# A hybrid-attention transformer block: where a gated product, four convolutions and nine operand splits stand

## The chip, the cores and the metric

The kernel runs on one core of a Trainium2 chip. The metric is the device time of one execution in microseconds; the median of several executions is given. TensorE is called PE here, with PEld for its weight loads; VectorE is DVE, ScalarE is ACT, GpSimd is POOL, and SP issues nearly all DMAs.

## What is computed

One transformer block over 512 tokens of 1024 features in float32: a modulation from a conditioning vector, a norm, a wide projection, a mixer of three kinds of heads, an output projection, a second norm and a gated feed-forward layer. Cut to what matters here:

```python
hn = (_rms(x, norm1_g[l]) * (1 + sc1) + sh1).astype(x.dtype)
proj = (hn @ w_in).astype(jnp.float32)
fq, fk, fv, ff, mq, mk, mv, mi, mf, mo, bq, bk, bv = jnp.split(proj, idx, axis=-1)
qk = jax.nn.silu(_causal_conv(jnp.concatenate([mq, mk], axis=-1), ml_conv_w, ml_conv_b))
mq, mk = jnp.split(qk, 2, axis=-1)
h_ml = _mlstm(_to_heads(mq, ML_HEADS), _to_heads(mk, ML_HEADS), ...)
...
gate, up = jnp.split(hn @ w_gate_up[l], 2, axis=-1)
x = x + g2 * ((jax.nn.silu(gate) * up) @ w_down[l])
```

The convolution has four taps along time, one weight per channel. There are four mLSTM heads, handled as two pairs, and 2816 feed-forward columns.

## The kernel before

Every float32 product is made of three products of split operands: a high part h (rounded, written by ACT) and a low part l = x - h (a subtraction), as `mm3` (hh, hl, lh) on PE. A weight tile therefore costs one ACT copy and one subtraction before PE can use it.

**Order of issue.** The tile framework places each engine's instructions itself while the program is built, by priority in the order of the text and by an estimate of when their inputs are ready; an instruction that stands late in the text may be placed early, where its engine would otherwise stand idle. What it has placed, an engine works off strictly in that order. A wrapper, `_InOrder`, can chain the instructions of an engine in the order of the text: while `in_order["V"][0]` and `in_order["S"][0]` are 1, those of DVE (`V`) and ACT (`S`) keep that order among themselves. What is issued after the switch is 0 again may still be placed between members of the chain. `SY` (the DMA issues) is chained from the feed-forward part on.

**First part.** After the norm, four 512-column products for the convolution (`gT` to `qkz[0..3]`; tiles 0 and 2 are the first pair of heads, 1 and 3 the second). Then come the projection groups of `add_group`, eight weight tiles each: `A` (values and gates of the mLSTM heads, tiles `Aw0` to `Aw7`), `F0`, `F1`, `F2`, `B0`, `B1`, `B2`, `E`, and the output projection. Their weight tiles are the steps of one loop: at step j the loop loads the tile three steps ahead, calls `attend`, and runs the calls of `extra[j]`. Group A is steps 0 to 7, F0 is steps 8 to 15. The low part of a weight tile is made on POOL for tiles 0, 2, 4, 6 (`WPG`) and on DVE for the others.

The four PSUM banks of a group are read by its `after`: for A, `after_a(t)` adds the gate bias (`gt`) and writes the values (`Vm`, high on ACT, low on DVE) for each of four token tiles. The banks of F0 are the same four, so F0 begins when `after_a(0)` has read its bank.

`conv(m)` makes a tile `cy` with one ACT operation, adds three taps on DVE, and applies Silu on ACT. It stands in `extra[CV + CVD*m]`, at steps 2, 4, 6, 8. `gates_1` to `gates_4` (steps 8 to 11) compute the log-sigmoid of the gates by a chain of small DVE operations (tile `gtmp`) with one Exp, sum it along time on PE (`pF`), and bring it into rows (`pR`, `RW`). `plan_mlstm(pr)` splits the convolved tiles (`mqh`, `mql`, `mkh`, `mkl`; `mql` on POOL), stacks them by DMA, and then weights scores by `E`, an Exp per tile.

**Feed-forward.** The 2816 columns are 11 strips of 256. Strips 1 to 10 use seven products instead of eight (`PHASES` 1, 2, 6, 5, 7, 4, 3), for which `sums(q)` forms four sums of weight tiles on DVE. In the trace they are: `r<-r,r` (r00 from r01, r00), `r1t<-r,r` (in later strips `r2t` and so on), `r<-r,r` (r01 from r11, r01) and `r<-r1t,r`. Each is split by `split` into `fw<strip><phase>h` on ACT and `...l` on DVE. Strip 0 is done plainly, by `plain(0)` for the first 256 tokens (two banks of tag g) and `plain(1)` for the others (two banks of tag t, which phase 5 of strip 1 needs next). `plain_glu(hb)` finishes a half: Silu of the gate bank into a tile `fps` on ACT, times the other bank on DVE, into `A0` (both called `A<-fp,fps` in the trace). The tile `fps` is one of 26 of tag `act`; in the text all 26 are taken when it is asked for, two of them by weights of `plain(1)` (`sph`, `spl`). Strip 1's weights are loaded by `load(1)`, strip 2's by `load(2)`, four DMAs each, in a fixed order.

Around the change, after `plain(1)`:

```python
load(1)
plain_glu(0)
in_order["V"][0] = in_order["S"][0] = 1
...
            if todo[ahead] == (1, 7):
                for g_ in range(2):
                    operand("s4", g_, s4[g_])
                plain_glu(1)
                in_order["V"][0] = in_order["S"][0] = 0
```

The loop prepares phases ahead of PE, so `prepare` runs for (1,1), (1,2), (1,6), (1,5), (1,7) before the first product of strip 1 is issued; (1,4), (1,3) and strip 2 follow with the chain off.

Of the kernel before, what the change touches and what calls it, by code (L numbers as in the profile page):

```python
# [12 lines left out]
ALU = mybir.AluOpType  # L13
# [62 lines left out]
WPG = (0, 2, 4, 6)  # L76
BLK = (3, 3)
BLKO0 = (2, 1)
BLKO1 = (3, 1)
CV = 2  # L80
CVD = 2
SB = 4
BIG = 1e30
ORDER1 = ""
# [47 lines left out]
def hybrid_block_kernel(  # L132
# [6 lines left out]
    V, S, G, TE, SY = nc.vector, nc.scalar, nc.gpsimd, nc.tensor, nc.sync  # L139
    dbg = dbg or {}  # L140
    in_order = {k: [1] for k in "VSGTY"}
    V, S, G, TE, SY = (_InOrder(tc, e, in_order[k]) for e, k in zip((V, S, G, TE, SY), "VSGTY"))

    def dump(key, src):
        if key in dbg:
            SY.dma_start(dbg[key], src)
# [5 lines left out]
    def bank(tag, name):  # L152
        return ps.tile([P, 512], F32, tag=tag, name=name, bufs=PSB[tag])

    def f32(ap):
        return ap.bitcast(F32)
# [59 lines left out]
    def mm3(o, ah, al, wh, wl, start, stop):  # L216
        TE.matmul(o, ah, wh, start=start, stop=False)
        TE.matmul(o, ah, wl, start=False, stop=False)
        TE.matmul(o, al, wh, start=False, stop=stop)
# [24 lines left out]
    def wload(src, n, name, lo=None, to=None):  # L244

        s_ = wp.tile([P, 512], F32, tag="ws", name=name + "s", bufs=WS)
        for a, o in (src if isinstance(src, list) else [(src, 0)]):
            if len(a.shape) == 3:
                w_ = a.shape[1] * a.shape[2]
                SY.dma_start(s_[:, o:o + w_].rearrange("p (a b) -> p a b", a=a.shape[1]), a)  # L250
            else:
                SY.dma_start(s_[:, o:o + a.shape[-1]], a)
        h_, l_ = to or (wp.tile([P, 512], F32R, tag="wh", name=name + "h"),
                        wp.tile([P, 512], F32R, tag="wl", name=name + "l"))
        S.activation(h_[:, :n], s_[:, :n], AF.Copy)
        (lo or V).tensor_tensor(l_[:, :n], s_[:, :n], f32(h_[:, :n]), op=ALU.subtract)
        return h_, l_


    with ExitStack() as s0:  # L260
# [6 lines left out]
        box = {}  # L267
# [143 lines left out]
    def add_group(name, kts, srcf, n, lhs, after, blk=BLK):  # L411
        box = {}

        def load(kt):
            box["w", kt] = wload(srcf(kt), n, f"{name}w{kt}", G if kt in WPG else V)

        cells = []
        first, last = kts[:blk[0]], kts[len(kts) - blk[1]:]  # L420
        cells = ([(kt, t) for t in range(NT) for kt in first]
                 + [(kt, t) for kt in kts[blk[0]:len(kts) - blk[1]] for t in range(NT)]
                 + [(kt, t) for t in range(NT) for kt in last])

        def cell(kt, t):
            if kt == kts[0]:
                box[t] = bank("g", f"{name}{t}")
            wh, wl = box["w", kt]
            ah, al = lhs(kt)
            tsl = slice(t * P, (t + 1) * P)  # L430
            mm3(box[t][:, :n], ah[:, tsl], al[:, tsl], wh[:, :n], wl[:, :n],
                kt == kts[0], kt == kts[-1])
            if kt == kts[-1]:
                after(t, box[t])

        def half(i, hb):
            for c_ in cells[4 * i + 2 * hb:4 * i + 2 * hb + 2]:
                cell(*c_)

        for i, kt in enumerate(kts):  # L440
            steps.append((lambda kt=kt: load(kt), lambda hb, i=i: half(i, hb)))
# [9 lines left out]
    def conv(m):  # L451
        w3 = prmT[:, 76 + m:77 + m]
        cb = prmT[:, 80 + m:81 + m]
        cy = hp.tile([P, 512], F32, tag="P1", name=f"cy{m}", bufs=SB)
        S.activation(cy, qkz[m], AF.Identity, scale=w3, bias=cb)
        for d in (1, 2, 3):
            wt = prmT[:, 64 + 4 * (3 - d) + m:65 + 4 * (3 - d) + m]
            V.scalar_tensor_tensor(cy[:, d:512], qkz[m][:, 0:512 - d], wt, cy[:, d:512],
                                   op0=ALU.mult, op1=ALU.add)
        S.activation(qkz[m], cy, AF.Silu)  # L460
        convolved.add(m)
        dump(f"qkz{m}", qkz[m])
# [93 lines left out]
    def gates_4(Mr):  # L556

        pM = bank("t", "pM")
        for t in range(NT):
            TE.transpose(pM[:, t * 4:(t + 1) * 4], Mr[:, t * P:(t + 1) * P], ident[0:4, 0:4])  # L560
        V.tensor_tensor(em, Fc[:, :, 0:4], pM[:, 0:16].rearrange("p (t g) -> p t g", t=NT), op=ALU.add)
        S.activation(em, em, AF.Exp, scale=-1.0)
        gs["em"] = em
# [55 lines left out]
    def pairt(name):  # L619
        return hp.tile([P, 512], F32R, tag="pair", name=name, bufs=4)  # L620
# [4 lines left out]
    def stack(qh, ql, kh, kl, bias=None):  # L625

        ops = []
        for j in range(2):
            js = slice(64 * j, 64 * j + 64)
            i_ = slot_no[0] = (slot_no[0] + 1) % NS  # L630
            mix, k1, q2, k2 = MIX[i_], K1[i_], Q2[i_], K2[i_]
            cpd(mix[0:64, :], qh[js, :])
            cpd(mix[64:128, :], ql[js, :])
            cpd(k1[0:64, :], kh[js, :])
            cpd(k1[64:128, :], kh[js, :])
            cpd(q2[0:64, :], qh[js, :])
            cpd(k2[0:64, :], kl[js, :])
            if bias is not None:
                bt, b0 = bias(j)
                cpd(k2[64:65, :], bt[b0:b0 + 1, :])  # L640
                cpd(k2[65:66, :], bt[b0 + 32:b0 + 33, :])
            ops.append((mix, k1, q2, k2))
        return ops
# [26 lines left out]
    def plan_mlstm(pr, s0):  # L670
        b = {}

        def prep():
            assert {pr, 2 + pr} <= convolved
            zq, zk = qkz[pr], qkz[2 + pr]
            qh, ql, kh, kl = (pairt(f"m{n}{pr}") for n in ("qh", "ql", "kh", "kl"))
            S.activation(qh, zq, AF.Copy)
            G.tensor_tensor(ql, zq, f32(qh), op=ALU.subtract)
            S.activation(kh, zk, AF.Copy, scale=0.125)
            V.scalar_tensor_tensor(kl, zk, 0.125, f32(kh), op0=ALU.mult, op1=ALU.subtract)  # L680
            b["ops"] = stack(qh, ql, kh, kl)
            b["num"] = hp.tile([P, NT, 2, 64], F32, tag="num", name=f"num{pr}", bufs=2)
            b["den"] = tiny.tile([P, NT, 2], F32, tag="den", name=f"den{pr}", bufs=2)
# [76 lines left out]
        def post_2():  # L760
# [3 lines left out]
            split_chunk(3 + pr, pt, V)  # L764

        at(s0 - MPREP, prep)
        for j in range(2):
            for kt in range(NT):
# [174 lines left out]
    for i in range(3):  # L943
        plan_softmax("B", i, 40 + 8 * i, gq8[:, 1:2], prmT[:, 87:88], lambda h: (AL, h), 5 + i)
    queue.sort(key=lambda e: e[:2])
    extra = {GT[0]: [g12], GT[1]: [g3], GT[2]: [g4], GT[3]: [lambda: gates_4(gs["M"])],
             len(steps) - len(OKT) + 2: [load_x1]}
    for m in range(4):
        extra.setdefault(CV + CVD * m, []).insert(0, lambda m=m: conv(m))

    def attend(now):
        while queue and (now is None or FIRST + queue[0][0] / RATE + max(0, queue[0][0] - 16) * SLOW <= now):
# [148 lines left out]
    def temp(name):  # L1101
        return act_tile(name, F32)
# [62 lines left out]
    def after(q, ph):  # L1165
        pb = pbk[q, BANK[ph]]
        if ph in (1, 6, 7):
            t_ = tmp[q, ph] = temp(f"u{q}{ph}")
            S.activation(t_, pb, AF.Copy)
        if ph == 2:  # L1170
            V.tensor_tensor(tmp[q, 1], pb, tmp[q, 1], op=ALU.add)
        elif ph == 7:
            pc = pbk[q, "C"]
            t_ = tmp[q, 5] = temp(f"u{q}5")
            V.tensor_tensor(t_, pc, tmp[q, 7], op=ALU.add)
        elif ph == 4:
            V.tensor_tensor(tmp[q, 7], tmp[q, 7], pb, op=ALU.subtract)
            glu(q, 1, tmp[q, 7], tmp[q, 5])
        elif ph == 3:
            V.tensor_tensor(tmp[q, 6], pb, tmp[q, 6], op=ALU.add)  # L1180
            glu(q, 0, tmp[q, 1], tmp[q, 6])
# [53 lines left out]
    def plain_glu(hb):  # L1235
        g_, u_ = pbank[hb]
        t_ = temp(f"fps{hb}")
        S.activation(t_, g_, AF.Silu)
        V.tensor_tensor(ffn["A"][0][:, :, 256 * hb:256 * hb + 256], u_.rearrange("p (a b) -> p a b", a=2),
                        t_.rearrange("p (a b) -> p a b", a=2), op=ALU.mult)  # L1240
# [27 lines left out]
    raw[1, "t2"] = fp.tile([P, 4, 256], F32, tag="raw", name="r1t", bufs=RAW)  # L1268
    ffn["A"][0] = fp.tile([P, 2, 512], F32, name="A0")
    load(1)  # L1270
    plain_glu(0)
    in_order["V"][0] = in_order["S"][0] = 1


# [26 lines left out]
    for i, (q, ph) in enumerate(run):  # L1301
        upto = todo.index(run[min(i + AHEAD, len(run) - 1)])
        while ahead <= upto:
            prepare(*todo[ahead])
            if todo[ahead] == (NQ - 1, 1):
                down_load(4)
            if todo[ahead] == (1, 7):
                for g_ in range(2):
                    operand("s4", g_, s4[g_])
                plain_glu(1)  # L1310
                in_order["V"][0] = in_order["S"][0] = 0
            ahead += 1
        product(q, ph)
        after(q, ph)
# [3 lines left out]
    for hf_ in range(2):  # L1318
# [17 lines left out]
        for t in range(NT):  # L1336
# [3 lines left out]
            for c_ in range(parts):  # L1340
                n = 512 // parts
# [45 lines left out]
```

## Time and profile before

| | |
|---|---|
| median of 3 runs | 693.05 us (691.87 to 693.31) |
| the profiled execution | 693.4 us, of which its span is 691.4 us |
| PE busy | 656.2 us, 95% |
| DVE busy | 518.6 us, 75% |
| ACT busy | 359.3 us, 52% |
| POOL busy | 101.0 us, 15% |
| mean granted PE clock | 0.984 of full |

All instructions carry line 115 (the wrapper), so they are told apart by their tiles. A row of a timeline gives start, duration, engine, operation, tile written from tiles read, shape, count, and in brackets the idle time of the engine just before and what ended it.

### The profile page before, as it was taken

Reading aid. Unit: us, or ns where it says so; the run is one execution under the profiler, and the core shown is the slowest. Engines: PE = TensorE matmul, PEld = TensorE weight load, DVE = VectorE, ACT = ScalarE, POOL = GpSimd, SP = SyncE. Lnnn points to the kernel's source line nnn. Section 1 sums busy time; section 2 is a strip of 40 time slices with the busy share of each in tenths; the row PEclk is TensorE's granted clock in tenths of the full one; section 3 lists DMA queues with packets and bytes.
Section 4 is the critical chain, followed back from the end, with each engine's and each line's share of the span. In section 5 each row is a group of like instructions: output and inputs, shape, how many; then the busy total and the mean of one; then the engine's idle time right before and its main releaser. Section 6 shows DMA issues by size and latency. Waiting matters only on the chain.

```text
span 691.4 us, 11769 instructions
## 1 busy us (share of the span) xinstructions
PE 656.2 (95%) x4238; PEld 593.0 (86%) x4238; DVE 518.6 (75%) x1028; ACT 359.3 (52%) x717; POOL 101.0 (15%) x136
## 2 busy tenths in 40 slices
PE   3999799999999999999995999999999999999997
PEld 2678678899999998778995999999999998788885
DVE  2549858779898899888758788877778999447313
ACT  3445536647867677646924454445445565325210
POOL 2006215242452455000000000000000000000000
PEclk9999879999999999999998999999999999999999
DMA  8985843576787676631806432233333227505101
GB/s 262 306 236 156 205 110 94 139 203 167 201 229 176 179 189 196 216 99 33 253 6 197 139 118 63 80 108 122 123 122 121 78 95 224 186 15 185 74 0 61
DMA packets 95549, 99.64 MB, mean 144 GB/s; under 512 B 8186, under 2 KB 70010, under 8 KB 95492
## 3 DMA queue, kind: packets, MB, share of 16 engines
q1 hardware_dynamic: 95492, 98.91, 49.1%
q8 instruction: 33, 0.54, 0.3%
q14 instruction: 24, 0.20, 0.1%
HBM read 84.15 MB, written 2.10 MB: 125 GB/s over the span
## 4 chain that ended last, share of the span: by engine, by line
PE 73%; DVE 15%; DMA 4%; issue 4%; ACT 3%; SPq 2%; DVEq 0%; ACTq 0%
PE d L115 14%; PE F L115 7%; PE B L115 6%; PE fp L115 3%; PE ol L115 3%; PE gT L115 2%; SPq L115 2%; PE mo L115 1%; PE f9A L115 1%; PE f8A L115 1%; PE f7A L115 1%; PE f6A L115 1%; PE f5A L115 1%; PE f4A L115 1%; PE f3A L115 1%
## 5 line engine op out<-in xcount | busy, mean ns | idle before, releaser
L115 ACT ACTIVATE ah<-A 128x512 fp32r<-128x512 f32 x44 | 25.6, 620 | 33.1 <-PE d L115 32.8
L115 DVE TENSOR_TENSOR al<-A,ah 128x512 fp32r<-128x512 f32 x44 | 29.0, 683 | 17.8 <-ACT ah L115 17.8
L115 DVE TENSOR_TENSOR r<-r,r 128x1024 f32<-128x1024 f32 x20 | 24.3, 1219 | 0.3
L115 DVE TENSOR_TENSOR fo<-d,g1b 128x512 f32<-128x512 f32 (+1 forms) x9 | 5.6, 630 | 17.9 <-PE d L115 17.8
L115 ACT ACTIVATE Fp<-Fs,Fmn 128x128 f32<-128x128 f32 (+3 forms) x24 | 12.7, 527 | 9.8 <-DVE Fmn L115 5.8
L115 ACT ACTIVATE Bp<-Bs,Bmn 128x128 f32<-128x128 f32 (+3 forms) x24 | 12.7, 528 | 6.6 <-DVE Bmn L115 4.1
L115 POOL TENSOR_SCALAR Fp<-Fp,Fls 128x128 f32<-128x128 f32 (+2 forms) x18 | 12.0, 668 | 26.4 <-DVE Fls L115 14.1
L115 DVE SCALAR_TENSOR_TENSOR m<-pc,b1sc,prmT 128x1 f32<-128x1 f32 x8 | 1.7, 218 | 18.5 <-PE pc L115 18.5
L115 PE MATMUL gT<-sq,ident 128*128 128x256 f32 x12 | 4.4, 546 | 10.4 <-ACT sq L115 10.4
L115 ACT ACTIVATE u<-u 128x512 f32<-128x512 f32 x20 | 12.5, 627 | 3.2 <-DVE u L115 3.0
L115 POOL TENSOR_SCALAR Bp<-Bp,Bls 128x128 f32<-128x128 f32 (+2 forms) x16 | 8.7, 546 | 34.4 <-DVE Bls L115 25.0
L115 DVE TENSOR_TENSOR A<-u,u 128x512 f32<-128x512 f32 x20 | 13.7, 683 | 0.0
L115 ACT ACTIVATE smh<-E 128x512 fp32r<-128x512 f32 (+3 forms) x16 | 7.5, 470 | 10.4 <-DVE E L115 10.3
L115 PEld LDWEIGHTS gT<-sq,ident 128*128 128x128 f32 x12 | 3.4, 291 | 11.0 <-issue 10.3
L115 DVE CUSTOM_DVE_ANT_0 Bs<-Bs,mask 128x128 f32<-128x128 f32 (+3 forms) x24 | 11.6, 491 | 1.6 <-PE Bs L115 1.6
L115 DVE TENSOR_TENSOR Bptl<-Bpt,Bpth 128x128 fp32r<-128x128 f32 (+3 forms) x24 | 11.5, 483 | 1.6 <-ACT Bpth L115 1.4
L115 ACT ACTIVATE Fpth<-Fpt 128x128 fp32r<-128x128 f32 (+3 forms) x24 | 10.5, 436 | 4.3 <-PE Fpt L115 4.1
L115 DVE CUSTOM_DVE_ANT_0 Fs<-Fs,mask 128x128 f32<-128x128 f32 (+3 forms) x24 | 11.7, 487 | 1.0 <-PE Fs L115 1.0
L115 PE MATMUL Bpt<-ident,Bp 128*128 128x128 f32 x60 | 10.8, 277 | 1.7 <-DVE Fyp L115 0.7
L115 POOL TENSOR_TENSOR sml<-E,smh 128x512 fp32r<-128x512 f32 (+1 forms) x8 | 8.6, 1080 | 24.9 <-ACT smh L115 20.0
L115 DVE TENSOR_TENSOR Fptl<-Fpt,Fpth 128x128 fp32r<-128x128 f32 (+3 forms) x24 | 11.6, 483 | 0.6 <-ACT Fpth L115 0.4
L115 ACT ACTIVATE Bpth<-Bpt 128x128 fp32r<-128x128 f32 (+3 forms) x24 | 10.3, 433 | 3.2 <-PE Bpt L115 2.8
(2324 smaller groups left out, 2835.1 us busy)
## 6 DMA issues: line engine op xcount, KB each, us to landing
r<-in_w_gate_up_dram SPq DMA_DIRECT2D x40, 512.0 KB, 4.7
dr<-in_w_down_dram SPq DMA_DIRECT2D x22, 512.0 KB, 5.2
ada<-in_w_ada_dram SPq DMA_DIRECT2D x16, 512.0 KB, 7.2
x<-in_x_dram SPq DMA_DIRECT2D x4, 512.0 KB, 4.6
w0s<-in_w_in_dram SPq DMA_DIRECT2D x8, 256.0 KB, 6.6
g10s<-in_w_ada_dram SPq DMA_DIRECT2D x8, 256.0 KB, 4.2
g11s<-in_w_ada_dram SPq DMA_DIRECT2D x8, 256.0 KB, 2.9
sc20s<-in_w_ada_dram SPq DMA_DIRECT2D x8, 256.0 KB, 4.5
```

The costliest lines, as they stand in the source:

```text
L115: r = f(*a, **k)
```

## The change

Five edits. `plain_glu(0)` moves from behind `load(1)` to behind the preparation of phase (1,7), ahead of the `s4` operands and `plain_glu(1)`, and so into the chained stretch. The convolutions are issued at steps 2 and 4 for tiles 0 and 2, and at steps 12 and 14 for tiles 1 and 3. The low parts of group A's tiles 0, 2, 4, 6 are made on DVE, and `mql` of both pairs too.

```diff
-CV = 2
-CVD = 2
+CVS = (2, 4, 12, 14)
@@ add_group
-            box["w", kt] = wload(srcf(kt), n, f"{name}w{kt}", G if kt in WPG else V)
+            box["w", kt] = wload(srcf(kt), n, f"{name}w{kt}", G if kt in WPG and name != "A" else V)
@@ plan_mlstm
-            G.tensor_tensor(ql, zq, f32(qh), op=ALU.subtract)
+            V.tensor_tensor(ql, zq, f32(qh), op=ALU.subtract)
@@ the steps
-    for m in range(4):
-        extra.setdefault(CV + CVD * m, []).insert(0, lambda m=m: conv(m))
+    for m, j in zip((0, 2, 1, 3), CVS):
+        extra.setdefault(j, []).insert(0, lambda m=m: conv(m))
@@ behind plain(1)
     load(1)
-    plain_glu(0)
     in_order["V"][0] = in_order["S"][0] = 1
@@ the loop over phases
             if todo[ahead] == (1, 7):
+                plain_glu(0)
                 for g_ in range(2):
                     operand("s4", g_, s4[g_])
                 plain_glu(1)
```

## Rows read from the trace of the kernel before

**Rows 1.** Stretches: us, busy (count) per engine; PE clock, DMA share, GB/s.

```profile
364.00:378.00 14.00, 7.06 (x34) 6.26 (x34) 13.26 (x13) 7.10 (x10) 0.00 (x0) 0.76 0.65 201
378.00:558.00 180.00, 180.00 (x1501) 179.84 (x1500) 150.50 (x159) 91.43 (x111) 0.00 (x0) 1.00 0.35 112
```

**Rows 2.** Timeline of PE, group F0 and the gates.

```profile
71.60 0.59 PE L115 MATMUL F<-F0w0h,hn0h 128*128 128x384 f32 x1 [2.88 <-DVE Vm L115]
...
74.87 0.44 PE L115 MATMUL F<-F0w0l,hn0h 128*128 128x384 f32 x1
75.16 0.33 PE L115 MATMUL F<-F0w0h,hn0l 128*128 128x384 f32 x1
75.33 0.33 PE L115 MATMUL F<-F0w1h,hn1h 128*128 128x384 f32 x1
...
84.81 0.61 PE L115 MATMUL pF<-gtmp,tri 128*128 128x10 f32 x4 [2.03 <-DVE gtmp L115]
```

**Rows 3.** Timeline of DVE, end of group A.

```profile
59.06 0.43 DVE L115 TENSOR_TENSOR Aw5l<-Aw5s,Aw5h 128x270 fp32r<-128x270 f32 x1
...
65.84 1.65 DVE L115 TENSOR_TENSOR F0w1l<-F0w1s,F0w1h 128x384 fp32r<-128x384 f32 x1
...
69.49 0.16 DVE L115 TENSOR_TENSOR gt<-A,gbias 128x14 f32<-128x14 f32 x1
...
71.65 0.74 DVE L115 SCALAR_TENSOR_TENSOR cy<-qkz,prmT,cy 128x509 f32<-128x509 f32 x1
...
72.84 0.16 DVE L115 TENSOR_TENSOR gt<-A,gbias 128x14 f32<-128x14 f32 x1
72.92 0.55 DVE L115 TENSOR_TENSOR F0w3l<-F0w3s,F0w3h 128x384 fp32r<-128x384 f32 x1
```

**Rows 4.** Timeline of POOL, the low part for the first pair.

```profile
65.33 1.74 POOL L115 TENSOR_TENSOR mql<-qkz,mqh 128x512 fp32r<-128x512 f32 x1
```

**Rows 5.** ACT: its table loads as a group (busy us, mean ns).

```profile
L115 ACT ACT_TABLE_LOAD x3 | 3.8, 1283 | 0.8 <-PEq L1376 0.8
```

**Rows 6.** Timeline of ACT, its longest gap while the gates are computed.

```profile
92.49 0.63 ACT L115 ACTIVATE RW<-rr 10x512 fp32r<-10x512 f32 x1 [8.75 <-DVE rr L115]
```

**Rows 7.** Timeline of ACT behind the plain strip.

```profile
364.08 0.60 ACT L115 ACTIVATE fps<-fp 128x512 f32<-128x512 f32 x1 [12.05 <-PE fp L115]
...
373.50 1.06 ACT L115 ACTIVATE fw17h<-r 128x1024 fp32r<-128x1024 f32 x1 [3.61 <-DVE r L115]
```

**Rows 8.** Timeline of DVE behind the plain strip.

```profile
364.71 0.69 DVE L115 TENSOR_TENSOR A<-fp,fps 128x512 f32<-128x512 f32 x1 [10.01 <-ACT fps L115]
...
366.57 1.23 DVE L115 TENSOR_TENSOR r1t<-r,r 128x1024 f32<-128x1024 f32 x1
367.71 1.22 DVE L115 TENSOR_TENSOR r<-r,r 128x1024 f32<-128x1024 f32 x1
...
369.98 1.22 DVE L115 TENSOR_TENSOR fw16l<-r1t,fw16h 128x1024 fp32r<-128x1024 f32 x1
...
372.25 2.35 DVE L115 TENSOR_TENSOR r<-r,r 128x1024 f32<-128x1024 f32 x2
```

**Rows 9.** DMA issues of `r` tiles, 334.9 to 341.5, and their time to landing.

```profile
L115 SPq DMA_DIRECT2D r<-in_w_gate_up_dram x5: 368/497/672, 335.7 to 340.2; - x5
...
DMA to landing us min/median/max: 6.2/7.2/7.4
```

**Rows 10.** The next issues of `r` tiles: timeline, wait (total, times, longest), landing.

```profile
362.70 1.47 SPq L115 DMA_DIRECT2D r<-in_w_gate_up_dram  x3
...
SPq L115 <- PE fp L115: 18.2, 1, 18.2
...
DMA to landing us min/median/max: 4.6/4.6/4.6
```

**Rows 11.** Timeline of PE behind the plain strip.

```profile
371.25 0.58 PE L115 MATMUL f1A<-os20h,fw16l 128*128 128x256 f32 x1 [1.46 <-DVE fw16l L115]
...
377.08 0.39 PE L115 MATMUL f1C<-os10h,fw15h 128*128 128x256 f32 x1 [0.50 <-ACT fps L115]
```

## The prediction

> **What bounds the kernel now.** I read the table of stretches first. From 378 to 558 us PE never rests [rows 1]: 180 us for 1501 matmuls, 0.12 us each, with DVE at 150 us. Nothing there can be won, and a stretch that only PE fills keeps whatever was won ahead of it. From 364 to 378 us PE works 7.06 of 14 us at a clock of 0.76, and DVE 13.26: here DVE sets the time [rows 1]. Then I asked the waits list for PE and looked each wait up in the timeline. In the first part there are two that matter: PE stands 2.88 us before group F0, until DVE has read the bank (Vm), and 2.03 us before pF, until DVE has the gates (gtmp) [rows 2]. The first also costs clock: the eleven F matmuls up to 74.87 start 0.327 us apart (3.27 us for ten intervals), the later ones 0.17 apart [rows 2], which loses 10 x 0.157 = 1.6 us. So the change touches two places: DVE's queue at 58 to 85 us, and DVE's queue at 354 to 378 us. They are priced apart.
>
> **The first part: splits and convolutions.** *Added to DVE ahead of the gates:* four splits of group A at 0.43 us and `mql` of the first pair, priced by a split of 384 columns (0.55) to 0.74 for an operation over 512 [rows 3]; I take 0.7. Sum 4 x 0.43 + 0.7 = 2.4 us. *Taken away:* up to six taps of the second pair at 0.74 [rows 3], 4.4 us. *Cheaper:* F0w1l took 1.65 us while POOL made `mql`, the same shape 0.55 later [rows 3, 4]. With `mql` off POOL that gives back 1.1 us; taps that ran beside POOL's other splits give back something too, which I don't count. So with no tap of the second pair ahead of the first `gt`, DVE reaches it 4.4 + 1.1 - 2.4 = 3.1 us earlier; with three of the six still there, 0.9 us earlier; with all six, 1.3 us later. The late convolutions are ready early, since their input is there before group A, and the framework fills gaps with what is ready, so some taps will stay; but gates and values now outrank them. I take 2.4 us, nearer the 3.1 because of the uncounted relief.
>
> F0 starts 2.1 us behind the first `gt` (69.49 to 71.60 [rows 2, 3]). Then PE waits 2.88 - 2.4 = 0.5 us instead of 2.88, and if so short a rest keeps the clock, the 1.6 us come back as well: PE would be 4.0 us ahead. But the next wait takes part of it. pF needs the gate chain, which runs from the last `gt` at 72.84 to 84.81, 12 us [rows 2, 3]; the last `gt` comes 2.4 us earlier, so pF does, and PE waits 2.03 + 1.6 = 3.6 us there instead of 2.03. The gain at pF is 2.4 us, not 4.0. Its ends: taps of the second pair that slip into the chain cost 0.74 each, so three of them take 2.2 and leave 0.2, and with all six back ahead of `gt` as well the gain is below nothing, -1.3; a chain shortened by as much as PE is ahead gives 4.0.
>
> The second `mql`, the stacking DMAs of the second pair (sixteen issues on SP, in the same queue as the weights of F1) and its splits follow the late convolutions. I cost them at nothing: they are first used by the scores of the second pair, at step 19, five steps behind the later convolution. If that cover were gone, F1's weight issues would stand behind them on SP.
>
> **A rule that speaks against it.** Today all four Silu stand ahead of the Exp of the gates, and the whole run has three table loads of 1.283 us [rows 5]. With the second convolutions behind the Exp, two or four more are due, 2.6 or 5.1 us of ACT. ACT has an idle stretch of 8.75 us while the gates are computed [rows 6], which holds either. I cost them at nothing there; outside it, up to 5.1 (rival three). The Trainium skill (ScalarE: Activation LUTs, "Table sets: the hidden batching unit") says to do all calls of one set before the other and puts a switch at about 2.66 us with its drain; by that figure, as an estimate, four loads would be 10.6 us, more than the idle stretch holds, and rival three would end near 701. The row has 1.283, and I go by it.
>
> **The second part: the gated product.** Today ACT's `fps` of the first half waits 12.05 us [rows 7], though its bank is full after half of the plain strip: its tile is the one of 26 that weights of `plain(1)` hold until 364.08. DVE waits 10.01 us for it, from 354.70 [rows 8], and the sums of strip 1 stand behind. The change moves two instructions (0.60 us on ACT, 0.69 on DVE [rows 7, 8]) behind the splits of phases 6, 5 and 7. The sums could then begin at 354.70: the five `r` DMAs issued up to 340.2 landed by 340.2 + 7.4 = 347.6 [rows 9].
>
> What is late next? Between `r1t` and `fw16l` DVE runs an `r<-r,r` at 367.71 [rows 8]. Strip 1 has only two sums of that form; one is r00, ahead of `r1t`, the other is r01, on which `fw17h` waited until 373.50 [rows 7], so it is the first of the pair at 372.25 [rows 8]. The one at 367.71 is strip 2's r00, put into the gap while ACT makes `fw16h`. It reads strip 2's r01, whose DMA is the sixth in order; that waits 18.2 us for PE, because its place in SBUF holds weights that `plain(1)` still reads, is issued at 362.70 and lands 4.6 us later, at 367.3 [rows 10]. Today that is hidden, since DVE comes there at 367.71. If this order stays, DVE stops behind `r1t` from 357 to 367.3, all of DVE's queue behind it, and `fw16l` starts 0.4 us earlier than today, not 10. The operation that moves stood ahead of all these, and nothing between them changes place, so I expect the order to stay. Against that 0.4, the moved `fps` adds up to 0.6 us on ACT ahead of the second `fps`, which frees the bank for f1C at 377.08 [rows 11]. Sum: 0.2 us lost; ends -0.4 (won) and +0.7, if DVE's 0.69 lands ahead of a split that PE waits for.
>
> Forecast against the profiled execution: 693.4 - 2.4 + 0.2 = 691.2 us, of which 2.0 lie outside its span. The median of the runs is 0.35 lower than that execution: 690.9 us. Its own range, from the ends above (4.0 and 0.4 won; 0.2 won and 0.7 lost, the least likely together), is 688.7 to 693.0.
>
> **Rivals.** *One: the sums really start early.* If strip 2's sum goes behind `fw17l` or at least behind `fw15l`, DVE needs r00, r1t, fw16l, fw15l, r01, fw17l from 354.70: six at 1.14 us (369.98 - 367.71 is two [rows 8]) and one wait of 1.06 for `fw16h`, done at 362.6. PE goes on at 364.08, f1A takes 24 x 0.12 = 2.9 us, the two `fps` follow on ACT meanwhile, and f1C starts at 367.0 instead of 377.08, 10.1 us earlier [rows 1, 7, 11]. With the 2.4: 693.05 - 12.5 = 680.5. For it: the DMAs are there, PE wants it. Against it: the row order just shown. *Two: nothing moves.* The framework hoists the late convolutions into the same gaps, the extra 2.4 us of splits eat the relief, or the gate chain eats the gain: 693.0. *Three, slower: the tables.* The two late Silu fall between the Exps of the first pair's decay tiles, after 97 us, and not into the idle stretch. Then four loads stand in the chain E - scores that PE waits on: 4 x 1.283 = 5.1 us against the 2.4, and 0.2: 695.9. It decides if either Silu is issued later than the first Exp of `E`.
>
> **How the numbers follow.** Forecast 0.45, rival one 0.22, rival two 0.18, rival three 0.15. Point: 690.9. A range of 8 in 10 has to take in rival one, so it goes from 680.0 to 694.4 (the 1.3 us that the first part can lose at its worst), leaving out most of rival three (0.12) and the deepest quarter of rival one (0.06). About 0.2%, 1.4 us, can be told from no change. Faster by more: 0.38 of the forecast's 0.45 and all of rival one, 0.60. Within: the rest of the forecast and most of rival two, 0.22. Slower: 0.18.
>
> **What would show it.** In the changed trace: the idle time of PE before the first F0 matmul, 0.5 us or less than 1, and F matmuls 0.17 apart from the start; pF near 82.4 with a wait of some 3.6 us; five or seven table loads, the extra ones before the first `E`. At the plain strip: DVE's `r<-r,r` in front of `fw16l` with an idle time of some 10 us that ends on a DMA. If instead that idle time is gone and f1C starts right behind f1A at the full clock, rival one holds. The forecast is wrong if PE waits for F0 as long as before, if `E` or the scores of the first pair start later than today relative to F0, or if DVE's place of strip 2's sum has moved.

## The result: 7.8 us faster, most of it from the first part

| | before | changed |
|---|---|---|
| median of 5 runs | 692.62 us (691.84 to 693.31) | 684.61 us (683.97 to 685.56) |
| profiled execution (its span) | 693.4 us (691.4) | 685.5 us (683.8) |
| PE busy | 656.2 us | 650.5 us |
| table loads on ACT | 3 | 7 |
| mean granted PE clock | 0.984 | 0.995 |

The ratio is 0.9888, 95% interval [0.9873, 0.9903], so 7.8 us less (6.7 to 8.8). In this part a difference in us is (ratio - 1) x 692, with its interval.

**Where it went, by places on PE.** The first matmul of each piece of work was looked up in both traces:

| first matmul on | before | changed | lead |
|---|---|---|---|
| F0's first weight tile | 71.6 | 69.9 | 1.7 |
| `pF` (gate sums) | 84.8 | 76.6 | 8.2 |
| `mb` (first decay tile's row) | 96.4 | 85.0 | 11.5 |
| F1's first weight tile | 104.4 | 94.3 | 10.1 |
| F2's first weight tile | 135.5 | 129.0 | 6.5 |
| output projection | 267.8 | 261.2 | 6.6 |
| plain strip (`fp`) | 340.2 | 333.4 | 6.8 |
| f1C | 377.1 | 369.4 | 7.7 |

The lead grows to 11.5 us until the first decay tile, 5 us are given back until F2, nothing changes for 200 us, and the second part adds 0.9. Each column is one execution: in the traces of e2 and e5 (below), which have the same first part, F2 starts at 127.6 and 127.7, so 1.4 of the 5 us belong to this execution of the changed kernel. The timeline of PE in the changed kernel answers to [rows 2] and [rows 11] (columns as there):

```profile
69.89 0.41 PE L114 MATMUL F<-F0w0h,hn0h 128*128 128x384 f32 x1 [0.72 <-DVE Vm L114]
...
76.60 0.61 PE L114 MATMUL pF<-gtmp,tri 128*128 128x10 f32 x4
...
84.95 0.46 PE L114 MATMUL mb<-RW,sel 64*128 64x512 f32 x1 [0.62 <-DVE RW L114]
...
109.80 0.46 PE L114 MATMUL mb<-RW,sel 64*128 64x512 f32 x1 [1.11 <-DVE E L114]
...
113.90 0.64 PE L114 MATMUL ms<-MIX,K 128*128 128x512 f32 x2 [1.37 <-DMA K<-mkh]
...
363.07 0.58 PE L114 MATMUL f1A<-os20h,fw16l 128*128 128x256 f32 x1 [5.54 <-DVE fw16l L114]
...
369.38 0.39 PE L114 MATMUL f1C<-os10h,fw15h 128*128 128x256 f32 x1 [0.50 <-ACT fps L114]
```

The wait ahead of `pF` is gone, and two waits of over 1 us between 104 and 118 us are new; the one at 113.90, for a DMA, does not come again in e2 and e5. The table of stretches shows both, and a thing that no list of waits shows, the clock (columns as in [rows 1]: busy us and count of PE, PEld, DVE, ACT, POOL, then the granted clock). Before:

```profile
72.00:86.00 14.00, 11.97 (x59) 11.09 (x58) 11.65 (x33) 7.22 (x17) 4.80 (x4) 0.87 0.78 196
86.00:104.00 18.00, 16.89 (x70) 13.90 (x69) 9.84 (x22) 7.02 (x21) 2.56 (x2) 0.73 0.45 112
104.00:160.00 56.00, 56.00 (x326) 49.40 (x327) 45.51 (x139) 33.30 (x101) 23.31 (x27) 1.00 0.53 138
```

Changed:

```profile
72.00:86.00 14.00, 13.38 (x79) 11.54 (x78) 10.87 (x29) 4.75 (x9) 3.31 (x3) 1.00 0.67 174
86.00:104.00 18.00, 17.82 (x92) 14.72 (x91) 15.40 (x32) 15.16 (x39) 5.07 (x5) 1.00 0.29 83
104.00:160.00 56.00, 52.96 (x315) 47.25 (x315) 47.13 (x148) 37.59 (x105) 22.59 (x27) 1.00 0.68 174
```

From 86 to 104 us PE was busy in both, 16.89 and 17.82 us, but did 70 matmuls in the one and 92 in the other: a busy PE at a clock of 0.73 looks like a full one. (It is not the same work, since the changed kernel is some 10 us ahead there.) DVE, at 9.84 of 18 us before, is at 15.40 now: the six taps of the second pair stand in this stretch.

**The gate chain.** The timeline of DVE before, from the last gate sums to their rows:

```profile
75.07 0.68 DVE L115 SCALAR_TENSOR_TENSOR mkl<-qkz,mkh 128x512 fp32r<-128x512 f32 x1
...
79.73 1.00 DVE L115 TENSOR_TENSOR F0w7l<-F0w7s,F0w7h 128x384 fp32r<-128x384 f32 x1 [1.29 <-ACT F0w7h L115]
80.65 0.98 DVE L115 TENSOR_SCALAR gtmp<-gtmp 128x40 f32<-128x40 f32 x1
81.66 3.10 DVE L115 SCALAR_TENSOR_TENSOR gtmp<-gtmp 128x40 f32<-128x40 f32 x9
...
87.89 0.20 DVE L115 COPY Fc<-pF 128x40 f32<-128x40 f32 x1 [2.26 <-PE pF L115]
...
91.78 0.68 DVE L115 COPY rr<-pR 10x512 f32<-10x512 f32 x1 [2.79 <-PE pR L115]
```

Changed:

```profile
66.46 0.16 DVE L114 TENSOR_TENSOR gt<-A,gbias 128x14 f32<-128x14 f32 x1
...
69.86 0.23 DVE L114 TENSOR_TENSOR gt<-A,gbias 128x14 f32<-128x14 f32 x2
...
74.26 0.19 DVE L114 TENSOR_SCALAR gtmp<-gtmp 128x40 f32<-128x40 f32 x1
74.48 2.07 DVE L114 SCALAR_TENSOR_TENSOR gtmp<-gtmp 128x40 f32<-128x40 f32 x9
...
78.55 0.20 DVE L114 COPY Fc<-pF 128x40 f32<-128x40 f32 x1 [1.59 <-PE pF L114]
...
79.85 0.68 DVE L114 COPY rr<-pR 10x512 f32<-10x512 f32 x1 [0.80 <-PE pR L114]
```

POOL in the kernel before, beside the end of the chain:

```profile
79.30 1.02 POOL L115 TENSOR_TENSOR F0w6l<-F0w6s,F0w6h 128x384 fp32r<-128x384 f32 x1 [4.96 <-ACT F0w6h L115]
80.34 1.25 POOL L115 TENSOR_TENSOR F1w0l<-F1w0s,F1w0h 128x384 fp32r<-128x384 f32 x1
81.55 1.28 POOL L115 TENSOR_TENSOR mql<-qkz,mqh 128x512 fp32r<-128x512 f32 x1
```

The first `gt` comes 3.0 us earlier than in [rows 3], and so does the last (72.84 to 69.9). From there to the end of the `gtmp` operations the chain takes 6.6 us instead of 12: `mkl` and two of the three `g` products of the modulation that stood in it are done ahead of it, in the room that the taps left, `F0w7l` with its wait of 1.29 us stands behind it, and the ten last `gtmp` operations take 2.3 us instead of 4.1. Before, POOL works beside those ten until 82.83; in the changed kernel its `F0w6l` starts at 77.49, behind them. From `pF` to `mb` it is 8.35 us instead of 11.6, with PE at the full clock: the two waits on PE are 1.59 and 0.80 us instead of 2.26 and 2.79. Sum at `mb`: 3 + 5.3 + 3.3, the 11.5 us of the table.

**The second part.** DVE, then PE (`f1A` and `f1C` above), do what the prediction described; the rows of DVE (before: [rows 8]):

```profile
349.07 1.23 DVE L114 TENSOR_TENSOR r1t<-r,r 128x1024 f32<-128x1024 f32 x1
359.52 1.22 DVE L114 TENSOR_TENSOR r<-r,r 128x1024 f32<-128x1024 f32 x1 [9.22 <-DMA r<-in_w_gate_up_dram]
...
361.80 1.22 DVE L114 TENSOR_TENSOR fw16l<-r1t,fw16h 128x1024 fp32r<-128x1024 f32 x1
```

### The profile page after: what moved, and what is told of

The parts are those of the page before. It is cut to its first block, busy times and chain, and to the rows that moved or that the text cites. A ratio compares the mean times of both kernels' runs of the same rounds, so it can differ in the third digit from the quotient of the medians.

```text
span 683.8 us, 11780 instructions
## 1 busy us (share of the span) xinstructions
PE 650.5 (95%) x4238; PEld 587.4 (86%) x4238; DVE 518.4 (76%) x1034; ACT 363.9 (53%) x721; POOL 95.7 (14%) x130
## 4 chain that ended last, share of the span: by engine, by line
PE 72%; DVE 15%; DMA 4%; ACT 4%; issue 4%; SPq 1%; DVEq 0%; ACTq 0%
PE d L114 14%; PE B L114 6%; PE F L114 6%; PE fp L114 3%; PE ol L114 3%; PE gT L114 3%; DVE g L114 1%; PE pc L114 1%; PE f9A L114 1%; PE f8A L114 1%; PE f7A L114 1%; PE f6A L114 1%; PE f5A L114 1%; PE f3A L114 1%; PE f4A L114 1%
## 5 line engine op out<-in xcount | busy, mean ns | idle before, releaser
L114 DVE TENSOR_TENSOR Bptl<-Bpt,Bpth 128x128 fp32r<-128x128 f32 (+3 forms) x24 | 11.5, 484 | 1.8 <-ACT Bpth L114 1.5
L114 DVE CUSTOM_DVE_ANT_0 Bs<-Bs,mask 128x128 f32<-128x128 f32 (+3 forms) x24 | 11.6, 491 | 1.6 <-PE Bs L114 1.5
L114 DVE TENSOR_TENSOR Fptl<-Fpt,Fpth 128x128 fp32r<-128x128 f32 (+3 forms) x24 | 11.6, 483 | 0.6 <-ACT Fpth L114 0.4
L114 ACT ACTIVATE row<-pc 128x256 f32<-128x256 f32 x8 | 3.1, 382 | 15.6 <-PE pc L114 15.6
```

The costliest lines, as they stand in the source:

```text
L114: r = f(*a, **k)
```

## The experiments

Each run stands against executions of the kernel before on the same chip. A trace is of one execution; where its time is more than 1 us off the run's median, the text gives it.

| run | what it is | ratio, 95% interval | us |
|---|---|---|---|
| e1_part2 | second part alone | 0.9990 [0.9977, 1.0002] | -0.7 |
| e2_part1 | first part alone | 0.9914 [0.9894, 0.9935] | -6.0 |
| e3_convs | later convolutions alone | 0.9974 [0.9959, 0.9990] | -1.8 |
| e4_splits | splits on DVE alone | 1.0011 [0.9992, 1.0030] | +0.8 |
| e9_convs_A | convolutions, group A's splits | 0.9985 [0.9977, 0.9993] | -1.0 |
| e13_convs_mql | convolutions, `mql` | 0.9950 [0.9933, 0.9968] | -3.5 |
| e15_chain_late | changed, gate chain lengthened | 0.9981 [0.9966, 0.9996] | -1.3 |
| e7_adjacent | e2, both later convolutions at step 14 | 0.9924 [0.9908, 0.9940] | -5.3 |
| e8_pin_before | before, strip 2's sum held back | 0.9984 [0.9975, 0.9993] | -1.1 |
| e14_part2_pin | second part, strip 2's sum held back | 0.9859 [0.9842, 0.9876] | -9.8 |
| e5_pinned | changed, strip 2's sum held back | 0.9770 [0.9754, 0.9787] | -15.9 |
| e12_pinned_eleven | e5, later convolutions at step 11 | 0.9840 [0.9825, 0.9855] | -11.1 |

### Each part alone

```diff
 e1_part2: kernel before, and
-    plain_glu(0)                 (behind load(1))
+                plain_glu(0)     (behind the preparation of (1, 7))
 e2_part1: changed kernel, and that line put back
```

> The kernel before with the second part alone: the gated product of the first half is issued behind the splits of phases 6, 5 and 7. Theory of the prediction: DVE keeps strip 2's r00 sum ahead of fw16l and stops there until the sixth r DMA has landed, so the time moves by -0.4 to +0.7 us against before, with an idle time of about 10 us on DVE that ends on a DMA. Rival one (the sums really start early): -10 us, f1C right behind f1A. A third reading, from the trace of the changed kernel, where f1C is 7.7 us earlier and the plain strip only 6.8: this part is worth -0.9 us.

> The changed kernel with the gated product of the first half put back to its old place: the first part alone (later convolutions of the second pair, splits of group A and mql on DVE). Prediction: -2.4 us against before (ends -4.0 and +1.3). From the trace of the changed kernel, in which group F2 and all after it start 6.5 us earlier: -6.6 us. If the two parts help each other, this one and the second part alone do not add up to -8.0.

The second part alone gave -0.7 us (-1.6 to +0.1), the first alone -6.0 (-7.3 to -4.5); they add up to -6.7, which the interval of the whole (-8.8 to -6.7) just takes in. The second part went as forecast, and the timeline of DVE in that run shows why it is worth so little:

```profile
355.53 1.23 DVE L115 TENSOR_TENSOR r1t<-r,r 128x1024 f32<-128x1024 f32 x1
365.95 1.23 DVE L115 TENSOR_TENSOR r<-r,r 128x1024 f32<-128x1024 f32 x1 [9.19 <-DMA r<-in_w_gate_up_dram]
```

DVE ends `r1t` 11 us earlier than in [rows 8] and then stands 9.19 us in front of strip 2's sum. The first part's forecast of -2.4 us was less than half of what it gave.

### The pieces of the first part

```diff
 e3_convs: kernel before, and
+CVS = (2, 4, 12, 14)
+    for m, j in zip((0, 2, 1, 3), CVS):
+        extra.setdefault(j, []).insert(0, lambda m=m: conv(m))
 e4_splits: kernel before, and
+ ... G if kt in WPG and name != "A" else V)
+            V.tensor_tensor(ql, zq, f32(qh), op=ALU.subtract)
 e9_convs_A:    e3 and the first of these two lines
 e13_convs_mql: e3 and the second
```

> The kernel before with the later convolutions alone; the splits of group A and mql stay on POOL. Theory that DVE's queue is what was relieved: the six taps of the second pair leave DVE ahead of the gates, so F0 and pF come at least as early as in the changed kernel, and the time is -6 to -7.5 us against before with seven table loads. Rival, that two engines working side by side is what cost the time (F0w1l took 1.65 us while POOL made mql): POOL still works there, so less than half of it comes, -1 to -3 us.

> The kernel before with the splits of group A and mql on DVE, convolutions where they were. Theory of DVE's queue: 2.4 us of work added ahead of the gates, 1.1 us given back by F0w1l, so +0 to +1.5 us against before, three table loads. Rival, that work on POOL beside DVE cost the time: -3 to -5 us.

> The changed kernel's first part without mql: later convolutions and splits of group A on DVE, mql still on POOL, the gated product where it was. If every POOL instruction over 512 columns beside DVE costs, F0w1l or a product g beside mql takes 1 us longer again, but only one such place is left ahead of the gates: -4 to -6 us against before, where the whole first part had -5.6 and the convolutions alone -1.8. Rival, that mql's place is the one that matters: -2 to -3.

> The other half of the run with group A's splits on DVE: later convolutions and mql on DVE, the splits of group A back on POOL, gated product in its old place. If mql is the piece of POOL work that matters, PE does not rest at pF and the time is -5 to -6 us against before. If any POOL operation over DVE's delays the gate chain beyond the place in PE's order that the framework gave pF, PE rests 1 us or more there, the clock falls behind it, and the time is -1 to -3 us.

The convolutions alone gave -1.8 us and the splits alone +0.8 (-0.6 to +2.1), together -6.0. e3 fell into the range of its rival (POOL beside DVE), e4 into that of its first theory (DVE's queue): neither reading holds for both, since each piece needs the other. In e3 the six taps are gone, and the first `gt` still comes at 69.96, as late as in [rows 3]. DVE, then POOL:

```profile
65.64 1.77 DVE L114 SCALAR_TENSOR_TENSOR g<-g10s,cs,g 128x512 f32<-128x512 f32 x1
...
68.00 1.37 DVE L114 TENSOR_TENSOR F0w1l<-F0w1s,F0w1h 128x384 fp32r<-128x384 f32 x1
...
69.96 0.16 DVE L114 TENSOR_TENSOR gt<-A,gbias 128x14 f32<-128x14 f32 x1
```

```profile
65.34 1.52 POOL L114 TENSOR_TENSOR mql<-qkz,mqh 128x512 fp32r<-128x512 f32 x1 [0.59 <-ACT mqh L114]
67.49 1.47 POOL L114 TENSOR_TENSOR F0w2l<-F0w2s,F0w2h 128x384 fp32r<-128x384 f32 x1 [0.62 <-ACT F0w2h L114]
```

A `g` that starts 0.3 us behind `mql` takes 1.77 us, and ends 0.55 us behind it; by itself it takes 0.74. `F0w1l` beside `F0w2l` takes 1.37 instead of 0.54. The framework also filled the place of the taps with two `g`. So the relief of DVE's queue is spent before the gates. (The Trainium skill, SBUF — State Buffer, "Who interferes with whom", says that a DVE instruction with two inputs in SBUF contends with one of POOL that reads SBUF, over a pair of ports under an exclusive lock. These rows agree in the main: `g` became 1.03 us longer, where `mql` ran on for 1.22 us.)

In e4 (its trace is of 695.46 us, the median is 693.02) it is the other way round. The first `gt` comes at 67.20, F0 starts at 70.11 after a rest of 0.28 us and at the full clock, so the 2.88 us of [rows 2] and the clock there are won; but the taps now stand inside the gate chain, and `pF` is where it was. DVE, then PE:

```profile
73.59 0.74 DVE L115 SCALAR_TENSOR_TENSOR cy<-qkz,prmT,cy 128x509 f32<-128x509 f32 x1
...
75.11 0.68 DVE L115 TENSOR_TENSOR mql<-qkz,mqh 128x512 fp32r<-128x512 f32 x1
...
79.12 1.41 DVE L115 TENSOR_TENSOR F0w7l<-F0w7s,F0w7h 128x384 fp32r<-128x384 f32 x1
```

```profile
70.11 0.41 PE L115 MATMUL F<-F0w0h,hn0h 128*128 128x384 f32 x1 [0.28 <-DVE Vm L115]
...
84.47 0.85 PE L115 MATMUL pF<-gtmp,tri 128*128 128x10 f32 x4 [1.46 <-DVE gtmp L115]
```

The wait in front of F0, the longest that the list of waits named in this stretch, was worth nothing alone.

e9 missed its range (-4 to -6) by 3 us and its rival's (-2 to -3) by 1. Up to `pF` it is nearly the changed kernel: F0 starts at 69.92, and in PE's order `pF` stands one matmul later. But with `mql` and its followers on POOL beside DVE the chain ends at 78.9 instead of 76.6, and PE, which comes to `pF` at 76.9, rests 2.02 us. e13 (trace of 690.24 us, median 688.59) lies between, with a rest of 1.02 us; its -3.5 us are between its two forecasts. The rows of `pF` on PE, e9, then e13, then e3, and behind them a stretch of e9, whose clock is the figure 0.50:

```profile
78.95 0.93 PE L114 MATMUL pF<-gtmp,tri 128*128 128x10 f32 x4 [2.02 <-DVE gtmp L114]
```

```profile
79.81 0.61 PE L114 MATMUL pF<-gtmp,tri 128*128 128x10 f32 x4 [1.02 <-DVE gtmp L114]
```

```profile
81.40 0.61 PE L114 MATMUL pF<-gtmp,tri 128*128 128x10 f32 x4 [2.19 <-DVE gtmp L114]
```

```profile
80.00:84.00 4.00, 4.00 (x15) 3.26 (x14) 0.46 (x3) 0.00 (x0) 0.00 (x0) 0.50 0.21 61
```

After the rest PE in e9 is at 0.50, which is the lower of its two levels (1.2 of 2.4 GHz), for the matmuls of `pF` and `pR`, on which DVE and ACT wait. From `pF` to `mb` it takes 11.5 us in e9, 11.6 before, 8.35 in the changed kernel. e3 rests as long, 2.19 us, but its clock falls later: `pF` runs at the full clock, the stretch from 84 to 86 us is at 0.52, and it is 8.9 us to `mb`. So the length of the rest does not say by itself what it costs. And e9, 2.45 us ahead of e3 at `pF`, is level with it at `mb` (90.40 and 90.31).

### Is it the rest, or the lateness of the gates?

```diff
 e15_chain_late: changed kernel, and in gates_1
+        for _ in range(9):
+            V.tensor_scalar(pl, pl, 1.0, None, op0=ALU.mult)
```

> The changed kernel with nine small operations more in the gate chain (each about 0.2 us on DVE, results unchanged), about 1.9 us in all. The framework knows of these and puts pF eight matmuls later in PE's order. Theory that what costs is PE's rest at pF and the clock behind it, not the lateness of the gates: PE rests less than 0.5 us there, the clock stays at 1.00 and the time is 0 to +1 us against the changed kernel. Rival, that each us by which the gates come later is lost one for one or more, as where mql stayed on POOL (gates 2.3 us later, 5 us lost): +2 to +5 us against the changed kernel.

A part of it came as the theory said. The nine operations took 2.78 us, PE rested 0.81 us at `pF` (under 0.5 expected), the clock stayed at 1.00 until 118 us, from `pF` to `mb` it was 8.3 us, and F1 started at 94.3 as in the changed kernel. But `mb` was 2.7 us late, and the time was 6.4 us above the changed kernel, so the theory falls and the rival's size, +2 to +5, was too small. The loss comes later. The waits of PE from 90 to 140 us, and one stretch:

```profile
PE mb L114 <- DVE E L114: 1.6, 1, 1.6
PE mo L114 <- ACT F1w7h L114: 1.5, 1, 1.5
PE mo L114 <- DVE den L114: 0.8, 1, 0.8
```

```profile
118.00:132.00 14.00, 13.87 (x66) 11.12 (x65) 12.06 (x30) 8.89 (x27) 3.57 (x3) 0.88 0.53 138
```

Between 104 and 120 us PE rests 3.9 us, for the decay tiles and the results of DVE and ACT, and the clock falls behind these rests. So two things seem to be worth time here: that `pF` and `pR` run at the full clock, for which e9 against e3 and the changed kernel speaks, and that the decay tiles start early, since PE waits for DVE and ACT from there to F2. Neither is isolated. The longer chain also moved other work: the first weight tile of F1 is used from 94.3 to 99.5 us in e15, to 106.0 in the changed kernel. And `mb` alone does not order the runs: it stands at 90.10 in the trace of e13 and at 87.65 in that of e15, while these two executions took 690.24 and 690.13 us.

### The table loads

```diff
 e7_adjacent: e2 (changed kernel, plain_glu(0) in its old place), and
-CVS = (2, 4, 12, 14)
+CVS = (2, 4, 14, 14)
 e12_pinned_eleven: e5 (below), and
+CVS = (2, 4, 11, 11)
```

> The changed kernel with both convolutions of the second heads at step 14, so that their two Silu stand side by side: five table loads instead of seven. Theory that the loads among the Exp of the decay tiles are what PE waits for between 98 and 115 us (3.2 us of waits in the changed kernel): 1.3 to 2.6 us better than the changed kernel. Rival, that those waits come from the work of the second pair itself (taps, splits and stacking DMAs behind the decay tiles on DVE and SP): no better, or up to 2 us worse since the first of the two comes later.

> The changed kernel with strip 2's first sum held back, and both convolutions of the second heads at step 11 instead of 12 and 14: their taps come ahead of the second row of decay tiles and their Silu side by side, five table loads instead of seven. Against the run with the sum held back alone (-15.6 us): if the waits of PE between 98 and 115 us come from the second pair's late work, -1 to -3 us more. If they come from DVE and ACT being full there in any order, no change, or up to 2 us worse since the first decay tiles then stand behind the taps.

In the changed kernel four loads are added, all behind the first decay tile (86.73), between Exps: at 94.92, 97.18, 104.49 and 106.85. The group of ACT answers to [rows 5]:

```profile
L114 ACT ACT_TABLE_LOAD x7 | 9.0, 1283 | 2.0 <-DVE cy L114 1.1 <-PEq L1375 0.8
```

The text above calls e7 the changed kernel, but in e7 the gated product stands in its old place. So e7 is to be compared with e2, the first part alone: -5.3 us (-6.4 to -4.2) with five loads, -6.0 (-7.3 to -4.5) with seven, no difference that the intervals show. Their traces agree too (e7's is of 685.24 us, its median 687.30; e2's of 685.23, median 686.27): F2 starts at 127.5 and 127.6, the plain strip at 332.4 and 332.6. e12, also with five, is 4.8 us behind e5, where at most 2 were forecast. Two loads fewer gained nothing in either. Both also moved the taps, so a small gain hidden by their place is not ruled out; in e12 the place costs more than any loads gave. There they stand ahead of the second row of decay tiles, and PE waits 1.65 us for a tile and does the next work at the low clock:

```profile
104.00:118.00 14.00, 12.08 (x42) 9.46 (x42) 9.80 (x32) 6.64 (x20) 6.90 (x9) 0.64 0.75 182
```

### The sum that stood in the way

```diff
 e8_pin_before: kernel before, and (e14: e1, and; e5: changed kernel, and)
@@ sums, for q == 2
-        V.tensor_tensor(r[0, 0], r[0, 1], r[0, 0], op=ALU.subtract)
+        d_ = V.tensor_tensor(r[0, 0], r[0, 1], r[0, 0], op=ALU.subtract)
+        tc.add_manual_dep(d_.ins, ffn["last"].name, ...)   # issue order only
@@ behind plain_glu(1)
+                ffn["last"] = V._last     (the last chained DVE instruction)
                 in_order["V"][0] = in_order["S"][0] = 0
```

> The kernel before with that dependence alone; the gated product of the first half stays ahead of the sums. Theory: DVE still stands until fps is there (364.7), and only the two sums of strip 2 leave its queue, 1.1 us ahead of fw16l and 1.1 us ahead of fw17l: -1 to -2.3 us against before. If the pin brought most of the gain by itself, -6 us or more, the move would not be needed.

> The kernel before with the second part and the dependence that holds strip 2's first sum back, without the first part. Theory: the move alone was worth -0.3 us and the dependence alone -1.1; together they take DVE's stop away and give what rival one of the prediction worked out, -9 to -10 us. Rival, that the two only add up: -1.4.

> The changed kernel with one dependence more: strip 2's first sum (its r00, which reads the sixth r DMA) may not be issued on DVE ahead of the last pinned instruction of strip 1, so fw16l, fw15l and fw17l stand directly behind r1t. Theory (the moved product is worth little because DVE stops at strip 2's sum): DVE runs from 348 to 357 us without the stop, f1A starts when the plain strip ends (357.2 instead of 363.1), and f1C, which then waits for the second fps alone, at about 360.5 instead of 369.4; 8 to 9 us better than the changed kernel, -16 to -17 us against before. Rival, that something else is late next (the fps tiles, fw14l, strip 2's own splits): f1A comes early but the stretch ends within 3 us of the changed kernel, -9 to -11.

All three came as expected: the dependence alone -1.1 us, with the moved product -9.8, and with the whole change -15.9 (-17.0 to -14.7), 8.1 better than the changed kernel. The first part alone (-6.0) and e14 add up to -15.8. In the changed kernel, too, two matmuls of f1A run at 357.1; PE then stands 5.54 us for `fw16l`. DVE and PE in e5, and its stretches:

```profile
350.85 1.23 DVE L114 TENSOR_TENSOR r<-r1t,r 128x1024 f32<-128x1024 f32 x1
352.00 1.22 DVE L114 TENSOR_TENSOR fw16l<-r1t,fw16h 128x1024 fp32r<-128x1024 f32 x1
```

```profile
357.66 0.28 PE L114 MATMUL f1A<-os20h,fw16h 128*128 128x256 f32 x1
...
360.86 0.38 PE L114 MATMUL f1C<-os10h,fw15h 128*128 128x256 f32 x1
```

```profile
340.00:364.00 24.00, 24.00 (x201) 23.87 (x201) 22.05 (x28) 11.35 (x17) 0.00 (x0) 1.00 0.27 92
364.00:378.00 14.00, 14.00 (x120) 14.00 (x118) 13.03 (x14) 6.68 (x8) 0.00 (x0) 1.00 0.72 219
```

PE no longer rests between the plain strip and strip 1, where [rows 1] had 7.06 of 14 us. At 676.54 us this kernel beats both: one dependence was missing for the moved product to do what it says.

## Why the prediction was right in sign and short in size

**F0's start: right, and of no weight.** The first `gt` came 3.0 us earlier (forecast 2.4), PE rested 0.72 us ahead of F0 (0.5, under 1), and its matmuls ran 0.17 us apart from the start. F0 stood 3.4 us behind that `gt`, not 2.1, because a `g` of 1.46 us and `mkl` came between, so it started only 1.7 us earlier. But e4 shows that these alone are worth nothing.

**The failed step is the term of the first part: 2.4 us, measured 6.0.** "The gain at pF is 2.4 us" rested on the chain keeping its 12 us. `pF` was forecast at 82.4 with a wait of 3.6; it ran at 76.60 with none. Two pieces were left out. The chain shrank to 6.6 us, because what had been inside it was moved ahead or behind by the framework, and because POOL no longer held DVE up; the row of `F0w1l` [rows 3] was counted for one split, where other operations beside POOL, those of the chain among them, were longer too. And the clock was priced at F0 alone (1.6 us), although `pF` had the same kind of rest in front of it: from 86 to 104 us the clock was 0.73 before and 1.00 after. How the 6.0 us divide between the shorter chain and the clock is not settled. Against that, the gain at `pF` was carried to the end without looking at 86 to 130 us, where PE now waits for others: 5 of the 11.5 us at `mb` went there (3.6 in e2 and e5).

**The table loads: the condition of rival three came true, its price did not.** Seven loads came, four of them among the decay tiles, where the main line expected all of them before the first `E`. The waits of PE from 98 to 115 us are 3.2 us, 1.4 of them for a DMA, and taking two of the loads out did not help (e7, e12). The rule of the Trainium skill (ScalarE: Activation LUTs, "Table sets: the hidden batching unit"; the 2.66 us stand under "What ACT_TABLE_LOAD costs") would have advised against this change; here no run shows that it cost anything.

**The second part: right in mechanism, and in size within its ends.** The forecast was 0.2 us lost, ends 0.4 won to 0.7 lost; measured 0.7 won (1.6 won to 0.1 lost). DVE stopped at strip 2's sum for 9.2 us, forecast some 10. The term that was off is the landing of the sixth `r`: 4.6 us by [rows 10], while in e1 the issue at 362.34 let the sum start at 365.95, 3.6 later. With 3.6 the prediction's own sum gives some 0.8 us won (1.4 less 0.6). Rival one, whose condition the change does not meet, had its price nearly right: 10.1 us worked out, 9.8 measured once the sum was held back.

So the time, 684.61, lies inside the range by way of the first part, and 4.1 us below the range that the forecast gave for itself (688.7 to 693.0). The wide range reached down to 680.0 for the sake of rival one, which did not happen: that it holds the result is luck.

## What to carry to other kernels

A wait of PE counts with what the clock does behind it and with who waits for PE then: look at the number of matmuls per stretch, not at the busy time, and price every rest behind which the trace shows a lower clock. When work is taken out of a queue in front of a chain, list what the scheduler will put into the gap and what will leave the chain, before taking the chain's length as given. An instruction that waits for a late DMA and may be placed freely is worth one dependence that holds it back.

## What the runs showed of the hardware

- DVE operations on SBUF that met one on POOL took up to three times as long (e3): 128x270 1.26 us instead of 0.43 (`Aw7l` from 63.80), 128x384 1.37 instead of 0.54, 128x512 1.77 instead of 0.74.
- Behind rests of PE in front of `pF` of 1.02 (e13), 1.46 (e4), 2.02 (e9), 2.03 (before) and 2.19 us (e3) the clock fell to about 0.50, in e9 at once, in e3 only from 84 us. Behind one of 0.81 (e15) it stayed at 1.00 until 118 us. In front of F0 rests of 1.13 (e9), 1.81 (e13) and 2.19 us (e3) left it at 1.00, one of 2.88 (before) did not. In the 4 us from 80 to 84, e9 did 15 matmuls and the changed kernel 21 (not the same work).
- Each ACT_TABLE_LOAD takes 1283 ns on ACT. Two fewer of them among Exps (e7 against e2) could not be found in the time.
